# First weight sums of two projections one step sooner, and the last mix's weights split ahead of the projection's end

## The chip, the cores and the metric

The kernel runs on one core of a Trainium2 chip. The core has a matrix engine (PE, with its weight loads shown apart as PEld), a vector engine (DVE), a scalar engine (ACT), a general engine (POOL) and DMA queues, most of whose transfers are issued by SP. Each engine works through its own queue of instructions in order; semaphores tie the queues together. The metric is the device time of one execution in microseconds.

## The reference

Two transformer blocks follow each other on 1024 tokens of width 1024, all in fp32. Of the first block the pool layer matters here, of the second the MLP:

```python
def multiscale_pool(u):                 # windows 2, 4, 8, 16 for four groups of 256 columns
    ...
        outs.append((c[:, 1:] - lower) / count - uf[:, :, gi])

def pool_layer(h, w_in, w_mix, scale, w_out):
    B, S, _ = h.shape
    u, z = jnp.split(h @ w_in, [POOL_WIDTH], axis=-1)        # 1024 -> 2048
    p = multiscale_pool(u)
    m = jnp.einsum('bsgc,gcd->bsgd', p, w_mix).reshape(B, S, POOL_WIDTH) * scale
    return (m * jax.nn.silu(z)) @ w_out
...
        m = rms_norm(h, norm_mlp[l])
        h = h + jnp.square(jax.nn.relu(m @ w_up[l])) @ w_down[l]     # 1024 -> 4096 -> 1024
```

Ahead of the pool layer stands a sliding window attention layer, ahead of the MLP a layer of neighbourhood attention and a gated recurrence.

## The kernel before, in words

**Matrix products.** A product of fp32 matrices is made of three matmuls: each operand is split into a rounded part ("hi") and the remainder ("lo"), and `mm3` adds hi by hi (L108), hi by lo and lo by hi (L110 and L111). So each operand of PE needs a cast, made by ACT, and a subtraction for the remainder, made by DVE (`split_evac`, L118 and L119) or by POOL (`split_w`, L79 and L80; `split_group`, L275 and L276; `split_b`, L118 with L119 on POOL). PE's output goes to one of eight banks, which ACT or DVE empties.

**Seven products in place of eight.** The large products are cut into 2 x 2 blocks and made from seven block products, with sums of blocks as operands: A11, A12, then S2, S1, S3, S4 and A22. The sums of blocks are made by DVE, of activations and of weights.

**`project_pairs`** (L327) makes a projection from 1024 columns in this way, in pairs of 128-column blocks of weights. It is used twice: for the pool layer's `w_in` (8 pairs, called at L959 with `NF` = 5) and for the MLP's `w_up` (16 pairs, called at L1912 with `NF` = 4). Pair p takes the products A11 and A12 first (`first_two`), then S2, S1, S3, S4 and A22 (`pair`). The weight sums of a pair are made from its raw weights r1 and r2 by four subtractions (`weight_sums`): the first three yield the operand tt of S2 and S1 whose second half ends the chain; then ACT casts tt (L275), POOL makes the remainder (L276) and PE can start S2.

Before the pairs run, the second half of the tokens is turned by PE (`turned`, L282, into banks) and `sums(j)`, for j = 0 to 3, makes from two banks the activation sums S2, S1 (both from A21 and A22), S3 and S4 with their splits: about a dozen instructions on DVE and six on ACT for each step. Beside each step j of 1 to 3 PE runs the two opening products of pair j, whose raw weights `split_first` loads and splits; with `NF` = 5 pair 4's come behind the last step. In the kernel before, `load_raw(0, ...)` asks for pair 0's raw weights behind step `NF` - 3, that is 2 in the pool projection and 1 in the up projection, and `weight_sums` runs on them behind step 3. Raw weights and their splits live in three buffers each (`wraw`, `whi`, `wlo`).

**The pool layer behind its projection.** `Pooled` takes the projection's results: even pairs give u, which is pooled and split, odd pairs give z, which goes through silu. After each second pair `mix(g, q)` multiplies one group with its 256 x 256 weights `w_mix`: `w_rows` loads the weights into a `wraw` buffer and splits them, PE makes four banks of six matmuls, DVE scales each and multiplies it by z (L942), and the four blocks and their sums S1 to S4 go to memory (L956) and are loaded back later as `ub` (L1001) for the out projection. The last mix, `mix(GO[3], 3)` at L992, comes behind the last pair. Between them in the text stand the loads of the out projection's weights (w11, w21, w22, w12), the splits of its first activation blocks (L981 for the casts, DVE for the remainders, held back to the projection's end by `issue_after(ended[...])`) and `split_b(w11)`, whose remainders are made by POOL. The out projection begins with A11 and A12, whose last part comes from the last mix directly; the next product takes S2, which is loaded back from memory.

**Order.** A scheduler writes each engine's queue: it goes through the program as written and places an instruction according to what it needs and when buffers come free; `issue_after` adds an edge by which an instruction comes behind another. So moving lines in the text moves rows on several queues.

Of the kernel before, what the change touches and what calls it, by code (L numbers as in the profile page):

```python
# [23 lines left out]
KT = D // P  # L24
# [6 lines left out]
def fused_kernel(tc, a, out, stop=None, dbg=None):  # L31
# [51 lines left out]
    def cols(w, c0):  # L83
        return (lambda r: r.rearrange("p (k c) -> p k c", k=KT), w[:, c0:c0 + P].rearrange("(k p) c -> p k c", p=P))
# [164 lines left out]
    def split_b(b_):  # L249
        res = []  # L250
        for i in range(2):
            hi, lo = [wpool.tile([P, 1024], F32R, name=n).rearrange("p (k c) -> p k c", k=2) for n in ("whi", "wlo")]
            split_evac(hi, lo, b_[i], nc.gpsimd)
            res.append((hi, lo))
        return res
# [71 lines left out]
    def project_pairs(w, col, npr, xx, sh, gcol, rows, a11, a12, stage, raw_tile, opened, res, w0, scaled, NF):  # L327
# [39 lines left out]

        def split_first(p):
            r_ = load_w(cols(w, col(p, 0))).rearrange("p (k c) -> p k c", k=KT)
            hv, lv = [wpool.tile([P, 1024], F32R, name=m).rearrange("p (k c) -> p k c", k=KT) for m in ("whi", "wlo")]  # L370
            for sl in (LO, HI):
                split_evac(hv[:, sl], lv[:, sl], r_[:, sl])
            wf[p] = hv, lv

        with tc.issue_after(scaled):
            split_first(1)

        def sums(j):
# [14 lines left out]
            h, l = xx.at(4 + j, H1)  # L393
            nc.scalar.activation(out=h, in_=pb, func=AF.Copy, scale=gb)
            fused(l, pb, gb, f(h), ALU.subtract)
            split_evac(sh[3][0][:, j, :], sh[3][1][:, j, :], s3)
# [4 lines left out]
            nc.vector.tensor_tensor(out=s2, in0=a_, in1=s2, op=ALU.subtract)  # L401
            split_evac(sh[4][0][:, j, :], sh[4][1][:, j, :], s2)

        banks = {0: [turned(rows[4:], k) for k in (0, 4)]}
        for j in range(4):
            if j < 3:
                banks[j + 1] = [turned(rows[4:], j + 1 + k) for k in (0, 4)]
            if 0 < j < NF:
                open_[j] = first_two(j, wf[j])
            sums(j)  # L410
            if j + 2 < NF:
                split_first(j + 2)
            if j + 3 == NF:
                r0 = [load_raw(0, i) for i in range(2)] + [raw()]
        ready = {1: weight_sums(*r0)}
# [390 lines left out]
    with ExitStack() as ph:  # L806
# [34 lines left out]
        class Pooled:  # L841
# [44 lines left out]
            def last(self, p, ps):  # L886
                c_ = self.dst(p, "21")
# [45 lines left out]
        def mix(g, q):  # L933

            wm, pp = w_rows(w_mix[g], 0, 2, 0, 256), pooled.pp.pop(q)
# [41 lines left out]
        with tc.issue_after(ended[0]):  # L977
# [6 lines left out]
            ops = split_b(w11)  # L984
# [1072 lines left out]
```

## Time and profile before

| | |
|---|---|
| Median of 3 runs | 2407.47 us (2406.76 to 2408.1) |
| Profiled execution, its own time | 2405.66 us |
| Its span on the core | 2403.8 us |
| Mean granted PE clock | 0.982 |
| Pool projection, first pair's preparation | 474 to 505 us of the span |
| Last mix and out projection | 670 to about 815 us |
| Up projection, first pair's preparation | 1767 to 1795 us |

The profile is of one execution; times count from the start of its span. A row of the timeline gives start, duration, engine, line, operation, output and inputs by the program's names, shapes, and how many instructions the row stands for; in brackets the engine's idle time before it and what released it. In the view of waits a row tells for one engine and line what it waited for, the total, how often, and the longest. Matmuls overlap: a row's duration is longer than the distance to the next start, and the distance is what one costs.

### The profile page before, as it was taken

What the parts mean: (1) busy time and instruction counts of PE and PEld (TensorE: products, weight loads), DVE (VectorE), ACT (ScalarE), POOL (GpSimd) and SP (SyncE); (2) the same over time, 40 slices, a digit from 0 to 9 for tenths busy, and PEclk for the clock granted to TensorE, in tenths of its full rate; (3) what the DMA queues carried; (4) which work ended last, traced back from release to release, by engine and by line L of the source; (5) the groups of instructions that cost most, each with busy time, mean ns of one, the idle gap of its engine ahead of it and who ended that gap; (6) DMA issues with size and microseconds to landing.
All of it is one profiled execution on the core that took longest, in us unless ns stands there. A gap on an engine that the chain in (4) does not pass through costs nothing. (4 is left out here: it accounts for less than half of the span.)

```text
span 2403.8 us, 32250 instructions
## 1 busy us (share of the span) xinstructions
PE 2293.1 (95%) x11910; PEld 1905.2 (79%) x11910; DVE 1509.5 (63%) x2730; ACT 1022.2 (43%) x1921; POOL 805.2 (33%) x529
## 2 busy tenths in 40 slices
PE   7999999989978999999999999999979999999997
PEld 6878778767767888888988888877768888888886
DVE  5566676787668355454165656759884444687775
ACT  5344451633335445454232322323565555533334
POOL 2112133234433244342122112126414444454455
PEclk9999999989989999999999999999989999999999
DMA  5111113423372322211111111358135444664331
GB/s 158 36 27 36 28 36 106 152 54 118 101 250 71 101 58 53 58 54 58 42 47 49 53 54 46 123 185 291 61 123 180 162 146 165 246 240 159 113 123 70
DMA packets 249230, 254.41 MB, mean 106 GB/s; under 512 B 61096, under 2 KB 183038, under 8 KB 244848
## 3 DMA queue, kind: packets, MB, share of 16 engines
q1 hardware_dynamic: 240256, 234.69, 30.1%
q10 hardware_dynamic: 8224, 16.00, 1.7%
q0 software_dynamic: 592, 1.65, 0.4%
q8 instruction: 94, 1.54, 0.3%
q14 instruction: 64, 0.52, 0.1%
HBM read 182.05 MB, written 70.25 MB: 105 GB/s over the span
## 5 line engine op out<-in xcount | busy, mean ns | idle before, releaser
L108 PE MATMUL mm<-xh,whi 128*128 128x512 f32 (+2 forms) x1616 | 622.1, 385 | 11.7 <-DVE z L226 2.6
L110 PE MATMUL mm<-xl,whi 128*128 128x512 f32 (+2 forms) x1616 | 615.7, 381 | 0.0
L111 PE MATMUL mm<-xh,wlo 128*128 128x512 f32 (+2 forms) x1616 | 612.7, 379 | 1.2 <-POOL wlo L80 1.2
L80 POOL TENSOR_TENSOR wlo<-wraw,whi 128x1024 fp32r<-128x1024 f32 (+1 forms) x99 | 238.6, 2413 | 730.2 <-ACT whi L79 668.0
L108 PEld LDWEIGHTS mm<-xh,whi 128*128 128x128 f32 x1616 | 305.9, 189 | 69.2 <-DVE z L226 3.6
L111 PEld LDWEIGHTS mm<-xh,wlo 128*128 128x128 f32 x1616 | 305.9, 189 | 59.7 <-POOL wlo L80 1.9
L110 PEld LDWEIGHTS mm<-xl,whi 128*128 128x128 f32 x1616 | 306.2, 189 | 51.0
L111 PE MATMUL mm<-whi,xl 128*128 128x512 f32 (+1 forms) x752 | 274.6, 365 | 0.0
L79 ACT CAST whi<-wraw 128x1024 fp32r<-128x1024 f32 (+1 forms) x99 | 101.2, 1023 | 263.8 <-PE mm L110 145.5
L110 PE MATMUL mm<-wlo,xh 128*128 128x512 f32 (+1 forms) x560 | 196.8, 351 | 2.4 <-POOL wlo L80 1.4
L108 PE MATMUL mm<-whi,xh 128*128 128x512 f32 (+1 forms) x560 | 197.1, 352 | 1.8 <-DVE x L504 1.0
L110 PE MATMUL mm<-wlo,xl 128*128 128x512 f32 x416 | 165.9, 399 | 9.5 <-POOL wlo L119 9.5
L108 PE MATMUL mm<-whi,xl 128*128 128x512 f32 x416 | 165.9, 399 | 9.5 <-DVE r L132 6.0
L276 POOL TENSOR_TENSOR wlo<-raw,whi 128x1024 fp32r<-128x1024 f32 (+1 forms) x59 | 123.2, 2089 | 131.1 <-ACT whi L275 131.0
L111 PEld LDWEIGHTS mm<-whi,xl 128*128 128x128 f32 x752 | 143.9, 191 | 22.4
L119 POOL TENSOR_TENSOR wlo<-wraw,whi 128x1024 fp32r<-128x1024 f32 x36 | 102.2, 2846 | 116.5 <-ACT whi L118 111.0
L110 PEld LDWEIGHTS mm<-wlo,xh 128*128 128x128 f32 x560 | 105.7, 189 | 17.0 <-POOL wlo L80 2.0
L108 PEld LDWEIGHTS mm<-whi,xh 128*128 128x128 f32 x560 | 105.8, 189 | 16.4 <-DVE x L504 1.4
L276 POOL TENSOR_TENSOR wlo<-wraw,whi 128x1024 fp32r<-128x1024 f32 (+1 forms) x28 | 68.9, 2466 | 146.2 <-ACT whi L275 118.7
L108 PEld LDWEIGHTS mm<-whi,xl 128*128 128x128 f32 x416 | 80.3, 193 | 28.8 <-ACT ea L1017 6.4
L110 PEld LDWEIGHTS mm<-wlo,xl 128*128 128x128 f32 x416 | 80.1, 193 | 28.1 <-POOL wlo L119 11.5
L1979 DVE TENSOR_TENSOR X<-X,mm 128x512 f32<-128x512 f32 x112 | 73.1, 681 | 37.5 <-PE mm L111 37.5
(435 smaller groups left out, 4583.6 us busy)
## 6 DMA issues: line engine op xcount, KB each, us to landing
wraw<-in_w_in_dram SPq DMA_DIRECT2D x48, 512.0 KB, 3.7
d_S<-st SPq DMA_DIRECT2D x64, 256.0 KB, 4.6
raw<-in_w_up_dram SPq DMA_DIRECT2D x30, 512.0 KB, 5.4
d_A<-st ACTq DMA_DIRECT2D x48, 256.0 KB, 2.0
fa<-d_S SPq DMA_DIRECT2D x10, 1024.0 KB, 4.6
fa<-d_A SPq DMA_DIRECT2D x9, 1024.0 KB, 5.8
wraw<-in_attn_w_in_dram SPq DMA_DIRECT2D x32, 256.0 KB, 3.0
xh<-in_w_down_dram SPq DMA_DIRECT2D x16, 512.0 KB, 5.4
```

The source lines that it names most:

```text
L79: nc.scalar.copy(out=hv[:, i:i + n], in_=view[:, i:i + n])
L80: nc.gpsimd.tensor_tensor(out=lv[:, i:i + n], in0=view[:, i:i + n], in1=f(hv[:, i:i + n]), op=ALU.subtract)
L108: nc.tensor.matmul(ps, lhsT=lh[0], rhs=rh[0], start=first and i == 0, stop=False, skip_group_check=chain)
L110: nc.tensor.matmul(ps, lhsT=lh[0], rhs=rh[1], start=False, stop=False, skip_group_check=chain)
L111: nc.tensor.matmul(ps, lhsT=lh[1], rhs=rh[0], start=False, stop=last and i == n - 1, skip_group_check=chain)
L119: return (lo_eng or nc.vector).tensor_tensor(out=lo, in0=src, in1=f(hi), op=ALU.subtract)
L276: nc.gpsimd.tensor_tensor(out=lv, in0=view, in1=f(hv), op=ALU.subtract)
L1979: added[:] = [nc.vector.tensor_tensor(out=dst, in0=dst, in1=banks[t], op=ALU.add)]
```

## The change

It has three parts.

1. In `project_pairs` the loads for `split_first` stand apart (`load_first`), and those of pairs 1 to 3 are asked for at the start. Pair 0's raw weights are asked for behind step 0, pairs 2 and 3 are split there, and pair 4 behind step 1. `weight_sums` runs behind step 2. `sums(j)` does the part that S2 and S1 need and returns the rest (the second half of A22's split, S3's split, S4's subtraction and split) as a function `rest`; it is called at once for j = 0 to 2, and for j = 3 behind the weight sums and the loop. The subtraction for S4 now goes through `vec` and so shows as L226 in place of L401.
2. The last mix's weights are loaded and split in `Pooled.last`, ahead of the last pair's last evacuation, in place of in `mix`.
3. `split_b` takes an engine; w11's remainders are made by DVE, in place of POOL, and not ahead of the last addition of the projection.

```diff
--- before.py
+++ after.py
@@ -246,11 +246,11 @@
             made[:] = [split_evac(t_[:, 2 * i:2 * i + 2, :], t_[:, 4 + 2 * i:6 + 2 * i, :], parts[i])]
         return t_
 
-    def split_b(b_):
+    def split_b(b_, eng=nc.gpsimd):
         res = []
         for i in range(2):
             hi, lo = [wpool.tile([P, 1024], F32R, name=n).rearrange("p (k c) -> p k c", k=2) for n in ("whi", "wlo")]
-            split_evac(hi, lo, b_[i], nc.gpsimd)
+            split_evac(hi, lo, b_[i], eng)
             res.append((hi, lo))
         return res
 
@@ -365,13 +365,20 @@
 
         open_, wf = {0: first_two(0, w0)}, {}
 
+        wr = {}
+
+        def load_first(p):
+            wr[p] = load_w(cols(w, col(p, 0))).rearrange("p (k c) -> p k c", k=KT)
+
         def split_first(p):
-            r_ = load_w(cols(w, col(p, 0))).rearrange("p (k c) -> p k c", k=KT)
+            r_ = wr.pop(p)
             hv, lv = [wpool.tile([P, 1024], F32R, name=m).rearrange("p (k c) -> p k c", k=KT) for m in ("whi", "wlo")]
             for sl in (LO, HI):
                 split_evac(hv[:, sl], lv[:, sl], r_[:, sl])
             wf[p] = hv, lv
 
+        for p in (1, 2, 3):
+            load_first(p)
         with tc.issue_after(scaled):
             split_first(1)
 
@@ -390,16 +397,21 @@
             split_evac(sh[2][0][:, j, :], sh[2][1][:, j, :], s2)
             fused(a21, pb, gb, a21, ALU.add)
             split_evac(*xx.at(j, H1), a21)
-            h, l = xx.at(4 + j, H1)
-            nc.scalar.activation(out=h, in_=pb, func=AF.Copy, scale=gb)
-            fused(l, pb, gb, f(h), ALU.subtract)
-            split_evac(sh[3][0][:, j, :], sh[3][1][:, j, :], s3)
+
+            def rest():
+
+                h, l = xx.at(4 + j, H1)
+                nc.scalar.activation(out=h, in_=pb, func=AF.Copy, scale=gb)
+                fused(l, pb, gb, f(h), ALU.subtract)
+                split_evac(sh[3][0][:, j, :], sh[3][1][:, j, :], s3)
+                vec(s2, a_, s2, ALU.subtract)
+                split_evac(sh[4][0][:, j, :], sh[4][1][:, j, :], s2)
+
             h, l = xx.at(4 + j, H0)
             a_, there = a12(j)
             if not there:
                 nc.gpsimd.tensor_tensor(out=a_, in0=f(h), in1=f(l), op=ALU.add)
-            nc.vector.tensor_tensor(out=s2, in0=a_, in1=s2, op=ALU.subtract)
-            split_evac(sh[4][0][:, j, :], sh[4][1][:, j, :], s2)
+            return rest
 
         banks = {0: [turned(rows[4:], k) for k in (0, 4)]}
         for j in range(4):
@@ -407,12 +419,22 @@
                 banks[j + 1] = [turned(rows[4:], j + 1 + k) for k in (0, 4)]
             if 0 < j < NF:
                 open_[j] = first_two(j, wf[j])
-            sums(j)
-            if j + 2 < NF:
-                split_first(j + 2)
-            if j + 3 == NF:
-                r0 = [load_raw(0, i) for i in range(2)] + [raw()]
-        ready = {1: weight_sums(*r0)}
+            rest = sums(j)
+            if j < 3:
+                rest()
+            if j == 0:
+                split_first(2)
+                split_first(3)
+                if NF > 4:
+                    load_first(4)
+                r0 = [load_raw(0, i) for i in range(2)]
+            if j == 1:
+                if NF > 4:
+                    split_first(4)
+                r0.append(raw())
+            if j == 2:
+                ready = {1: weight_sums(*r0)}
+        rest()
         for p in range(4, NF):
             open_[p] = first_two(p, wf[p])
         opened()
@@ -884,6 +906,8 @@
                     self.steps()
 
             def last(self, p, ps):
+                if p == 7:
+                    self.wm = w_rows(w_mix[GO[3]], 0, 2, 0, 256)
                 c_ = self.dst(p, "21")
                 if p % 2:
                     ended[:] = [nc.scalar.activation(out=c_, in_=ps, func=AF.Silu).ins, added[0].ins]
@@ -932,7 +956,7 @@
 
         def mix(g, q):
 
-            wm, pp = w_rows(w_mix[g], 0, 2, 0, 256), pooled.pp.pop(q)
+            wm, pp = pooled.wm if q == 3 else w_rows(w_mix[g], 0, 2, 0, 256), pooled.pp.pop(q)
             zs = [pooled.t.pop((2 * q + 1, j)) for j in range(2)]
             m = {(j, h): zs[j][:, h * 512:h * 512 + 512] for j in range(2) for h in range(2)}
             for j, h in ((0, 0), (1, 0), (0, 1), (1, 1)):
@@ -981,7 +1005,8 @@
                 nc.scalar.copy(out=h_, in_=r_)
                 with tc.issue_after(ended[1]):
                     vec(l_, r_, f(h_), ALU.subtract)
-            ops = split_b(w11)
+            with tc.issue_after(ended[1]):
+                ops = split_b(w11, nc.vector)
         X = Rows([raw_tile().rearrange("p k c -> p (k c)") for _ in range(4)], None, None)
 
         def load_x(h, ch):
```

Line numbers move by some twenty: L385, L401, L942 and L981 before are L392, L226, L966 and L1005 after.

DVE's queue in the pool projection, at the third and fourth step of the sums (`fused` is L385 before and L392 after; `wraw<-wraw` is a weight sum of pair 0; `ea<-ea,mm` adds the opening products of a pair). Before:

```order
L401 TENSOR_TENSOR u<-u 128x512
L119 TENSOR_TENSOR wlo<-wraw,whi 128x512
L385 SCALAR_TENSOR_TENSOR z<-mm,vecs,sum 128x512
L119 TENSOR_TENSOR s4l<-u,s4h 128x512
L226 TENSOR_TENSOR ea<-ea,mm 128x512
L385 SCALAR_TENSOR_TENSOR sum<-mm,vecs,z 128x512
L385 SCALAR_TENSOR_TENSOR z<-mm,vecs,z 128x512
L119 TENSOR_TENSOR s3l<-z,s3h 128x512
L119 TENSOR_TENSOR s2l<-sum,s2h 128x512
L119 TENSOR_TENSOR xl_5018<-z,xh_5017 128x512
L385 SCALAR_TENSOR_TENSOR xl_5018<-mm,vecs,xh_5017 128x512
L401 TENSOR_TENSOR sum<-sum 128x512
```

After:

```order
L226 TENSOR_TENSOR u<-u 128x512
L226 TENSOR_TENSOR wraw<-wraw 128x512
L392 SCALAR_TENSOR_TENSOR z<-mm,vecs,sum 128x512
L119 TENSOR_TENSOR s4l<-u,s4h 128x512
L226 TENSOR_TENSOR wraw<-wraw 128x512
L226 TENSOR_TENSOR ea<-ea,mm 128x512
L226 TENSOR_TENSOR wraw<-wraw 128x512 x2
L392 SCALAR_TENSOR_TENSOR sum<-mm,vecs,z 128x512
L392 SCALAR_TENSOR_TENSOR z<-mm,vecs,z 128x512
L119 TENSOR_TENSOR s3l<-z,s3h 128x512
L119 TENSOR_TENSOR s2l<-sum,s2h 128x512
```

Pair 0's four weight sums stand among the first rows of the last step; before, the first of them came right behind the rows shown. The splits of the opening weights (`wlo<-wraw,whi`) moved ahead of this place.

ACT's queue at the end of the last pair and the last mix (L876 and L889 before, L898 and L913 after, are the evacuations of the last pair; L79 is the cast of the mix's weights; `whi<-wraw` at L118 are w11's). Before:

```order
L876 COPY z<-mm 128x512 x2
L882 ACTIVATE z<-z 128x512 x2
L889 ACTIVATE z<-mm 128x512
L981 CAST xh_6331<-raw 128x1024
L981 CAST xh_6331<-raw 128x512
L981 CAST xl_6332<-raw 128x1024
L981 CAST xl_6332<-raw 128x512
L118 CAST whi<-wraw 128x1024 x2
L79 CAST whi<-wraw 128x512
```

After:

```order
L898 COPY z<-mm 128x512
L79 CAST whi<-wraw 128x512
L898 COPY z<-mm 128x512
L904 ACTIVATE z<-z 128x512 x2
L913 ACTIVATE z<-mm 128x512
L1005 CAST xh_6337<-raw 128x1024
L1005 CAST xh_6337<-raw 128x512
L1005 CAST xl_6338<-raw 128x1024
L1005 CAST xl_6338<-raw 128x512
L118 CAST whi<-wraw 128x1024 x2
```

The cast of the mix's weights went from behind w11's to between two evacuations of the last pair.

DVE's queue at the same place (`raw` holds the activation blocks loaded back, `w` is in w21, w22 and w12's sums, L942 and L966 are the four results of the last mix, `sum<-z` is its S2). Before:

```order
L226 TENSOR_TENSOR xh_6331<-raw,xh_6331 128x512
L226 TENSOR_TENSOR xl_6332<-raw,xl_6332 128x1024
L226 TENSOR_TENSOR xl_6332<-raw,xl_6332 128x512
L241 TENSOR_TENSOR w_6326<-w_6326,w_6325 128x1024 x2
L942 SCALAR_TENSOR_TENSOR z<-mm,vecs,z 128x512 x2
L119 TENSOR_TENSOR xh_6331<-z,xh_6331 128x512
L942 SCALAR_TENSOR_TENSOR z<-mm,vecs,z 128x512
L119 TENSOR_TENSOR xl_6332<-z,xl_6332 128x512
L226 TENSOR_TENSOR z<-z 128x512
L942 SCALAR_TENSOR_TENSOR z<-mm,vecs,z 128x512
L226 TENSOR_TENSOR z<-z 128x512
L226 TENSOR_TENSOR sum<-z 128x512
```

After:

```order
L226 TENSOR_TENSOR xh_6337<-raw,xh_6337 128x1024
L226 TENSOR_TENSOR xh_6337<-raw,xh_6337 128x512
L226 TENSOR_TENSOR xl_6338<-raw,xl_6338 128x1024
L226 TENSOR_TENSOR xl_6338<-raw,xl_6338 128x512
L119 TENSOR_TENSOR wlo<-wraw,whi 128x1024 x2
L119 TENSOR_TENSOR xh_6337<-z,xh_6337 128x512
L966 SCALAR_TENSOR_TENSOR z<-mm,vecs,z 128x512 x3
L119 TENSOR_TENSOR xl_6338<-z,xl_6338 128x512
L226 TENSOR_TENSOR z<-z 128x512
L241 TENSOR_TENSOR w_6332<-w_6332,w_6331 128x1024
L226 TENSOR_TENSOR z<-z 128x512
L226 TENSOR_TENSOR sum<-z 128x512
```

w11's two remainders are in DVE's queue now, and the two L241 rows, ahead of the mix's results before, went to between the sums and behind S2 (the second is the row after the last one shown).

## The prediction

> **What bounds the kernel now.** I read the page's first table, then PE's waits, then the granted clock by stretch, then the rows round each long wait.
>
> ```profile
> span 2403.8 us, 32250 instructions
> PE 2293.1 (95%) x11910; PEld 1905.2 (79%) x11910; DVE 1509.5 (63%) x2730; ACT 1022.2 (43%) x1921; POOL 805.2 (33%) x529
> ```
>
> PE is busy for 95% of the span, so a change that gives it no less work can only win back PE's idle time, and the clock it loses behind idle time. The view of waits (engine, line, waited for: us in total, times, longest) between 440 and 820 us, where the pool layer runs, and between 1750 and 2080 us, where the up projection runs, holds the waits that the edits touch:
>
> ```profile
> PE mm L108 <- ACT whi L79: 6.0, 1, 6.0
> PE mm L108 <- DVE r L132: 6.0, 1, 6.0
> PE mm L111 <- POOL wlo L80: 5.7, 1, 5.7
> PE mm L108 <- ACT whi L275: 5.2, 1, 5.2
> ```
> ```profile
> PE mm L108 <- ACT whi L275: 9.5, 1, 9.5
> ```
>
> The L275 waits are for pair 0's first weight sums (place A in the pool projection, place B in the up projection). The L79 and L80 waits are for the last mix's weights, and the 6.0 under r L132 comes in the out projection behind it (place C). The windows view (start:end, then length and busy time of PE, PEld, DVE, ACT, POOL, then PEclk, DMA share, GB/s) shows what comes after such waits:
>
> ```profile
> 496.00:513.00 17.00, 10.58 (x31) 7.63 (x30) 14.28 (x18) 4.66 (x8) 6.36 (x3) 0.70 0.06 15
> 604.00:612.00 8.00, 6.12 (x28) 4.72 (x27) 6.67 (x8) 4.11 (x6) 2.61 (x2) 1.00 0.23 67
> 670.00:690.00 20.00, 8.30 (x24) 5.78 (x23) 12.53 (x10) 7.17 (x10) 8.29 (x3) 0.66 0.48 163
> ```
>
> The clock falls to 0.70 and 0.66 behind the waits of A and C, and stays at 1.00 over the 1.88 us wait in the middle row (its row is below). Full-rate starts of matmuls lie 0.23 us apart, half-rate ones 0.43; so 13 half-rate ones behind A's wait cost 2.5 us, and 10 behind C's second wait 2.0.
>
> **Place A: pair 0's sums one step sooner.** Columns: start, duration, engine, operation, count, idle time before.
>
> ```profile
> 606.84 0.50 PE L108 MATMUL mm<-s2h,whi 128*128 128x512 f32 x1 [1.88 <-ACT z L876]
> 473.89 0.69 DVE L401 TENSOR_TENSOR u<-u 128x512 f32<-128x512 f32 x1
> 500.02 2.02 DVE L226 TENSOR_TENSOR wraw<-wraw 128x512 f32<-128x512 f32 x3
> 501.46 2.51 ACT L275 CAST whi<-wraw 128x1024 fp32r<-128x1024 f32 x3 [2.51 <-DVE wraw L226]
> 502.56 0.79 PE L108 MATMUL mm<-s2h,whi 128*128 128x512 f32 x1 [5.21 <-ACT whi L275]
> 502.59 6.36 POOL L276 TENSOR_TENSOR wlo<-wraw,whi 128x1024 fp32r<-128x1024 f32 x3 [12.99 <-ACT whi L275]
> 504.99 0.80 PE L111 MATMUL mm<-s2h,wlo 128*128 128x512 f32 x1 [1.21 <-POOL wlo L276]
> ```
>
> The chain is: third weight sum on DVE (second of the three at 500.02, done about 501.4), cast on ACT, remainder on POOL (2.4 us after 502.59, at 504.99), and PE's first matmul with wlo. DVE works without a break from 473.89 to 501.4: 41 instructions in 27.5 us, 0.67 each. In the changed order 32 stand ahead of the same sum, since what the last step defers goes behind it; 9 fewer is 6.0 us, so the sum ends near 495.4. But ACT must first evacuate that step's first product, and PE now comes later: two subtractions for weights stand ahead of the additions that free the transposes' bank, 2 x 0.67 less slack, which I put at 1.15 us. PE's last opening product then ends at 498.7 instead of 497.35 (502.56 less 5.21), and the cast starts near 496.7, 4.8 us sooner. wlo is there at 500.2, again 4.8 sooner. PE waits about 1 us, less than the 1.88 us that left the clock alone, so the 2.5 us of half rate goes too. **A: 4.8 + 2.5 = 7.3.** Bounds: 8.9 if both waits and the half rate go entirely (5.21 + 1.21 + 2.5), 2 if ACT's cast gains only about half and the clock still falls. What DVE defers (S3's and S4's remainders) is needed by products that PE starts only after S2 and S1, some 96 matmuls or 22 us later, which hides it. The raw weights are asked for earlier from a queue that moves 15 GB/s in that stretch, at no cost that I can see.
>
> **Place B: the same code in the up projection.**
>
> ```profile
> 1766.23 0.69 DVE L401 TENSOR_TENSOR st<-fa,st 128x512 f32<-128x512 f32 x1
> 1769.51 0.50 PE L108 MATMUL mm<-xh,whi 128*128 128x512 f32 x1 [1.25 <-ACT st L388]
> 1790.17 1.29 DVE L226 TENSOR_TENSOR wraw<-wraw 128x512 f32<-128x512 f32 x2
> 1792.07 6.38 POOL L276 TENSOR_TENSOR wlo<-wraw,whi 128x1024 fp32r<-128x1024 f32 x3 [55.46 <-ACT whi L275]
> 1794.48 0.79 PE L111 MATMUL mm<-s2h,wlo 128*128 128x512 f32 x1 [1.27 <-POOL wlo L276]
> ```
>
> From 1766.23 to the end of the third sum (first of the two at 1790.17, done at 1790.85) DVE has 37 instructions; 29 are left ahead of it, 8 x 0.67 = 5.3 us sooner. The addition that frees the bank stands behind three more instructions, so PE's first product of that step starts up to 2 us later and DVE waits some 0.6 us of it out: 5.3 - 0.6 = 4.7, and POOL's remainder and the matmul at 1794.48 move with it. PE still waits here, over 4 us in all, so the half rate behind it (6 matmuls, 1.2 us) stays. **B: 4.7.** Bounds: 12.0 (9.53 + 1.27 + 1.2) and 1.5, if the later bank costs DVE all of its 2 us and another 2.
>
> **Place C: the last mix's weights, and w11's remainder on DVE.**
>
> ```profile
> 670.13 0.39 PE L111 MATMUL mm<-xh,wlo 128*128 128x512 f32 x1
> 675.87 0.62 ACT L79 CAST whi<-wraw 128x512 fp32r<-128x512 f32 x1
> 681.14 2.24 POOL L80 TENSOR_TENSOR wlo<-wraw,whi 128x512 fp32r<-128x512 f32 x1
> 683.44 0.79 PE L111 MATMUL mm<-sum,wlo 128*128 128x512 f32 x1 [5.68 <-POOL wlo L80]
> 690.91 0.39 PE L108 MATMUL mm<-whi,xh 128*128 128x512 f32 x1
> 712.03 0.39 PE L108 MATMUL mm<-whi,xl 128*128 128x512 f32 x1
> 715.32 0.50 PE L110 MATMUL mm<-wlo,xl 128*128 128x512 f32 x1 [2.22 <-POOL wlo L119]
> 744.76 0.77 PE L108 MATMUL mm<-whi,xl 128*128 128x512 f32 x1 [5.99 <-DVE r L132]
> 672.12 1.83 DVE L226 TENSOR_TENSOR xh<-raw,xh 128x1024 fp32r<-128x1024 f32 x2 [3.59 <-ACT xh L981]
> 673.87 1.82 DVE L226 TENSOR_TENSOR xl<-raw,xl 128x1024 fp32r<-128x1024 f32 x2
> 675.60 6.66 DVE L241 TENSOR_TENSOR w<-w,w 128x1024 f32<-128x1024 f32 x2
> 694.93 0.68 DVE L226 TENSOR_TENSOR sum<-z 128x512 f32<-128x512 f32 x1
> 695.64 0.32 SPq L956 DMA_DIRECT2D d_mS<-sum  x1
> 701.36 0.80 SPq L1001 DMA_DIRECT2D ub<-d_mS  x2
> 706.21 2.00 ACT L118 CAST xl<-ub 128x1024 fp32r<-128x1024 f32 x2 [4.00 <-DMA ub<-d_mS]
> 711.95 6.64 POOL L119 TENSOR_TENSOR wlo<-wraw,whi 128x1024 fp32r<-128x1024 f32 x2 [11.83 <-ACT whi L118]
> 739.58 3.29 DVE L119 TENSOR_TENSOR xl<-ub,xl 128x1024 fp32r<-128x1024 f32 x1
> 743.95 0.67 DVE L226 TENSOR_TENSOR z<-z,mm 128x512 f32<-128x512 f32 x1
> ```
>
> The mix's cast (0.62 us) and its remainder (2.24) move to about 661-663, ahead of the last evacuation; both fit beside PE's last product. PE runs on from 670.5: 24 matmuls x 0.23 end the mix at 676.0, where now the out projection starts at 690.91. w11's two remainders cost DVE 1.2 us each (the 1024-column part of the 1.83 row) in place of 6.1 on POOL and come about 677, a wait of half a microsecond. So PE is 14 us ahead there. It cannot keep them. Its first out products (690.91 to 712.03, 21.1 us) would end near 697.7, and the next one needs S2, which goes through DRAM: sum at 694.93, store, load at 701.36, cast at 706.21, POOL at 711.95, matmul at 715.32. That is 19.7 us from the sum's end to the matmul, and the change touches none of it. How much sooner is the sum? By PE alone, 681 (4.7 us after the mix, as now). By DVE, from 672.1: 3.65 for the four subtractions, 2.4 for w11, 3.3 for the half of L241 ordered ahead, nine 128x512 operations at 0.7: 15.7 us, so 688. I take 688, since all of these stand in its queue ahead of the sum: PE resumes at 688 + 19.7 = 707.7, after a **new wait of about 10 us** at the S2 product, with half rate behind it as now.
>
> From there to 744.76 PE now takes 29.4 us, 23.5 of them work and 5.99 the wait for a bank, which the addition at 743.95 frees. The second half of xl's remainder (3.29) and one addition (0.8 with its gap) go behind it: 29.4 - 4.1 = 25.3, so the gate opens at 733.0. **C: 744.76 - 733.0 = 11.7**. Bounds: 25.6 if the four waits (6.01, 5.68, 2.22, 5.99) and the half rate behind them (5.7) all go; 4 if the sum is no earlier and only DVE's 4.1 us are saved.
>
> The wait at that gate is then about 1.8 us, and I leave the 2.1 us of half rate behind it in. The Trainium skill ("TensorE: Matmul & The Clock Gate", section "HAM oscillation") says 'The abstract rule is "no PE-idle gaps >~3.4µs."' By that rule the 2.1 us go as well and the time would be 2381.7. But behind the 1.25 us wait at 1769.51 ten matmuls ran at half rate, so this trace does not bear the rule out and I do not use it.
>
> **Sum.** 7.3 + 4.7 + 11.7 = 23.7. The profiled execution's 2403.8 becomes 2380.1. The median lies 3.67 above that span: **2383.8 us**.
>
> **Rivals.** *More is kept:* S2's sum comes when PE allows, at 681. Then PE resumes at 700.7, C is 18.7, and the time 2376.8. For it: most of DVE's remainders could run while PE mixes; against it: the order puts them first. *Less is kept:* C's wait comes back nearly whole at the S2 product, because POOL's and DVE's work collide (the 6.66 us for two L241 is 3.3 each), the sum stays at 695, C is 4 and A and B at 60%: 11, or 2396. *Slower:* PE falls to half rate at 676 and the short waits that follow keep it there, so the 216 matmuls up to the gate take 0.20 us more each: 43 - 23.7 = 19 slower, 2427. It decides from about 120 such matmuls. Against it: after each wait seen, the clock came back within 6 to 13 matmuls. *It does not do what it says:* the sums are not sooner because the raw weights land late; the order shows them asked for a whole step ahead, and then only C is left, 2396.
>
> **Chances.** Forecast, 2378 to 2391: 0.60. More kept: 0.14. Less kept, or C alone: 0.19. No change 0.03; slower 0.04. The range 2373 to 2397 takes in both neighbours and leaves out the bounds' far corners. What a measurement of this kernel can tell from no change is about 0.2%, 4.8 us; so faster 0.93, same 0.03, slower 0.04.
>
> **What would show it.** In A a wait of about 1 us before the S2 product and the clock above 0.9 there; in B the wait of 9.53 down to 3 to 5; the L275 casts near 496.7 and, in the old count, 1786. In C no wait at the mix, a wait of 8 to 11 us some 27 us after the mix began, released by POOL's wlo at L119, and the gate's wait near 2. It is wrong if the clock stays low between them, or if a wait appears after 760 us, where I expect every product to move unchanged.

## The result, and the profile after

| | before | after |
|---|---|---|
| Median | 2407.11 us (4 runs) | 2394.57 us (4 runs, 2391.29 to 2395.45) |
| Ratio of the times | | 0.9946, 95% interval 0.9929 to 0.9963 |
| Span of the profiled execution | 2403.8 us | 2393.6 us |

The change makes the kernel 12.5 us faster, and by the interval between 8.9 and 17.1. The forecast was faster by 23.7, to 2383.8. The direction held and the size is half: 2394.57 lies inside the wide range of 2373 to 2397, but outside the 2378 to 2391 that the forecast gave most of its chance. The page's first lines, after:

```profile
span 2393.6 us, 32247 instructions
PE 2290.5 (96%) x11910; PEld 1904.0 (80%) x11910; DVE 1509.4 (63%) x2732; ACT 1021.5 (43%) x1921; POOL 802.7 (34%) x527
```

PE has the same 11910 matmuls. To see where time went, the same matmul is looked up in both executions and its starts compared; a negative shift means earlier than before.

| Matmul | before | after | shift |
|---|---|---|---|
| pool projection, ahead of place A | 440.16 | 440.57 | +0.4 |
| A: pair 0, S2, first matmul with wlo | 504.99 | 500.50 | -4.5 |
| A: pair 0, S3, first | 512.87 | 505.63 | -7.2 |
| A: pair 1, S2, second | 521.26 | 521.90 | +0.6 |
| mix of the first group | 540.11 | 537.91 | -2.2 |
| last pair, S3 | 660.46 | 658.30 | -2.2 |
| C: out projection, second product | 701.84 | 685.29 | -16.6 |
| C: product with S2, first with wlo | 715.32 | 706.24 | -9.1 |
| C: product behind the bank's wait | 744.76 | 734.07 | -10.7 |
| ahead of B | 1691.79 | 1681.93 | -9.9 |
| B: pair 0, S2, first matmul with wlo | 1794.48 | 1780.04 | -14.4 |
| B: pair 1, A22, first | 1820.82 | 1809.84 | -11.0 |
| last matmul | 2390.32 | 2380.12 | -10.2 |

At each of the three places a gain appears that is about as large as forecast, and part of it, in A nearly all, is gone a few microseconds later. In A and B the view of PE's waits (engine, line, waited for: total, times, longest) names what took it back; first 440 to 820 us, then 1750 to 2080 us:

```profile
PE mm L108 <- ACT whi L118: 7.0, 1, 7.0
...
PE mm L108 <- DVE u L226: 5.4, 2, 5.0
PE mm L108 <- DVE w L128: 5.0, 1, 5.0
```
```profile
PE mm L108 <- DVE st L1853: 3.6, 3, 2.6
PE mm L108 <- ACT whi L275: 3.2, 1, 3.2
```

The waits of 6.0 us for L79 and 5.7 for L80 are gone; that for L275 is 3.2 us in place of 9.5 in B, and there is none in A. The waits for DVE's u (L226) and st (L1853, L1828 before) were 0.5 and 0.8 us in all before: these are additions, by which DVE takes a product out of a bank that PE's next product needs. The 7.0 us is the wait for S2 that the forecast had put at about 10.

**Place A after**, from the timelines of PE, DVE and POOL:

```profile
500.50 0.50 PE L111 MATMUL mm<-s2h,wlo 128*128 128x512 f32 x1 [1.34 <-POOL wlo L276]
505.63 0.39 PE L108 MATMUL mm<-s3h,whi 128*128 128x512 f32 x1
516.19 0.79 PE L108 MATMUL mm<-xh,whi 128*128 128x512 f32 x1 [4.95 <-DVE u L226]
509.15 0.68 DVE L226 TENSOR_TENSOR raw<-raw 128x512 f32<-128x512 f32 x1
509.92 2.86 DVE L226 TENSOR_TENSOR wraw<-raw 128x512 f32<-128x512 f32 x1
512.82 2.71 DVE L226 TENSOR_TENSOR wraw<-raw,wraw 128x512 f32<-128x512 f32 x1
515.46 0.67 DVE L226 TENSOR_TENSOR u<-u,mm 128x512 f32<-128x512 f32 x1
509.86 2.39 POOL L276 TENSOR_TENSOR wlo<-wraw,whi 128x1024 fp32r<-128x1024 f32 x1 [4.90 <-ACT whi L275]
512.21 2.77 POOL L276 TENSOR_TENSOR wlo<-raw,whi 128x1024 fp32r<-128x1024 f32 x1
```

The matmul at 516.19 is the first of pair 0's last product, A22, which goes into a bank that this addition has to read first; it starts at 515.46. (The expectations below call that product pair 1's first; it is pair 0's A22.) Ahead of it in DVE's queue stand pair 2's weight sums, which nobody needs for another pair's length. The first takes 0.68 us, the next two 2.86 and 2.71: both began after a subtraction on POOL had begun, and end 0.5 us behind its end (POOL 512.25 and 514.98, DVE 512.78 and 515.53). That is what is seen if DVE does nothing while POOL works and then takes its usual time. DVE had stood still beside the remainders of pair 0 before the change too; new are the 4.2 us beside those of pair 1, which before found DVE idle and waiting for PE. The Trainium skill ("SBUF — State Buffer", section "SBUF: two separate sides") says that an operation of GpSimd and a DVE operation with two inputs in SBUF share a pair of ports as an exclusive lock, held for the whole instruction. These rows agree with that, and group_dve below bears it out: without POOL's subtractions the same rows take 0.69 us.

**Place B after** shows the same pattern at pair 0's A22: a weight sum stretched from 0.68 to 2.71 us beside POOL's subtraction, the addition right behind it, and PE's matmul. At pair 1's A22, 16 us later, additions again stand behind weight sums of a later pair; here one of them waits 1.18 us for its raw weights from memory:

```profile
1789.30 2.84 POOL L276 TENSOR_TENSOR wlo<-wraw,whi 128x1024 fp32r<-128x1024 f32 x1 [1.77 <-ACT whi L275]
1789.97 2.71 DVE L226 TENSOR_TENSOR wraw<-raw 128x512 f32<-128x512 f32 x1
1792.61 0.67 DVE L1853 TENSOR_TENSOR st<-st,mm 128x512 f32<-128x512 f32 x1
1793.34 0.50 PE L108 MATMUL mm<-xh,whi 128*128 128x512 f32 x1 [0.69 <-DVE st L1853]
1807.17 0.69 DVE L226 TENSOR_TENSOR wraw<-raw 128x512 f32<-128x512 f32 x1 [1.18 <-DMA raw<-in_w_up_dram]
1809.11 1.28 DVE L1853 TENSOR_TENSOR st<-st,mm 128x512 f32<-128x512 f32 x2
1809.84 0.50 PE L108 MATMUL mm<-xh,whi 128*128 128x512 f32 x1 [2.60 <-DVE st L1853]
```

**Place C after:**

```profile
681.35 2.88 DVE L226 TENSOR_TENSOR z<-z 128x512 f32<-128x512 f32 x1
684.14 0.68 DVE L226 TENSOR_TENSOR sum<-z 128x512 f32<-128x512 f32 x1
690.66 0.79 SPq L1026 DMA_DIRECT2D ub<-d_mS  x2
697.11 1.99 ACT L118 CAST xl<-ub 128x1024 fp32r<-128x1024 f32 x2 [5.53 <-DMA ub<-d_mS]
706.24 0.80 PE L110 MATMUL mm<-wlo,xl 128*128 128x512 f32 x1 [0.82 <-POOL wlo L119]
729.37 3.30 DVE L119 TENSOR_TENSOR xl<-ub,xl 128x1024 fp32r<-128x1024 f32 x1
734.07 0.76 PE L108 MATMUL mm<-whi,xl 128*128 128x512 f32 x1 [5.02 <-DVE w L128]
```

S2's sum ends at 684.8 in place of 695.6, and its way through memory to PE's first matmul with wlo takes 21.4 us where it took 19.7: the load now takes 6.5 us from its issue to the cast, where it took 4.9. So of the 14 us that PE had gained at the mix, 7 were left. And at the bank behind it a remainder of 3.30 us, beside POOL's subtraction, still stands ahead of the addition, as it did before:

```profile
728.89 2.70 POOL L119 TENSOR_TENSOR wlo<-w,whi 128x1024 fp32r<-128x1024 f32 x1 [5.86 <-ACT whi L118]
```

### The profile page after: what moved, and what is told of

It reads as the page before. It is cut to its first block, busy times and chain, and to the rows that moved or that the text cites. A ratio compares the mean times of both kernels' runs of the same rounds, so it can differ in the third digit from the quotient of the medians.

```text
span 2393.6 us, 32247 instructions
## 1 busy us (share of the span) xinstructions
PE 2290.5 (96%) x11910; PEld 1904.0 (80%) x11910; DVE 1509.4 (63%) x2732; ACT 1021.5 (43%) x1921; POOL 802.7 (34%) x527
## 5 line engine op out<-in xcount | busy, mean ns | idle before, releaser
L80 POOL TENSOR_TENSOR wlo<-wraw,whi 128x1024 fp32r<-128x1024 f32 (+1 forms) x99 | 235.8, 2385 | 739.9 <-ACT whi L79 676.0
L79 ACT CAST whi<-wraw 128x1024 fp32r<-128x1024 f32 (+1 forms) x99 | 101.1, 1023 | 264.0 <-PE mm L110 146.0
L110 PE MATMUL mm<-wlo,xl 128*128 128x512 f32 x416 | 164.5, 396 | 10.7 <-POOL wlo L119 10.7
L119 POOL TENSOR_TENSOR wlo<-wraw,whi 128x1024 fp32r<-128x1024 f32 x34 | 95.3, 2807 | 103.4 <-ACT whi L118 98.0
L226 DVE TENSOR_TENSOR st<-st 128x512 f32<-128x512 f32 x64 | 63.2, 1008 | 56.7 <-ACT st L1928 55.6
```

The lines of the kernel that those rows point to most:

```text
L79: nc.scalar.copy(out=hv[:, i:i + n], in_=view[:, i:i + n])
L80: nc.gpsimd.tensor_tensor(out=lv[:, i:i + n], in0=view[:, i:i + n], in1=f(hv[:, i:i + n]), op=ALU.subtract)
L110: nc.tensor.matmul(ps, lhsT=lh[0], rhs=rh[1], start=False, stop=False, skip_group_check=chain)
L119: return (lo_eng or nc.vector).tensor_tensor(out=lo, in0=src, in1=f(hi), op=ALU.subtract)
L226: return nc.vector.tensor_tensor(out=out_, in0=x_, in1=y_, op=op)
```

## The experiments

All ran with the kernel before beside them, whose median lay between 2407.1 and 2408.6; differences from the changed kernel are between medians. Each kernel ran 4 to 10 times, and its executions spread over 2 to 9 us, so where two intervals overlap, the difference of the two kernels is not certain. Line numbers in rows are each kernel's own.

| Kernel | median | ratio to before, 95% |
|---|---|---|
| changed kernel | 2394.57 | 0.9946 (0.9929 to 0.9963) |
| only_mix | 2400.12 | 0.9969 (0.9957 to 0.9981) |
| only_sums | 2401.26 | 0.9975 (0.9965 to 0.9985) |
| mix_pool | 2398.78 | 0.9965 (0.9953 to 0.9977) |
| sums_behind_adds | 2391.32 | 0.9934 (0.9919 to 0.9949) |
| s2_first | 2391.39 | 0.9933 (0.9918 to 0.9948) |
| group_dve | 2389.35 | 0.9923 (0.9908 to 0.9938) |
| adds_s2 | 2389.44 | 0.9925 (0.9910 to 0.9940) |
| adds_s2_x | 2389.18 | 0.9925 (0.9908 to 0.9941) |
| all_four | 2391.75 | 0.9934 (0.9922 to 0.9947) |
| group_s2_x | 2385.72 | 0.9907 (0.9893 to 0.9920) |
| all_four_p3 | 2385.76 | 0.9905 (0.9890 to 0.9920) |
| out_dve | 2380.64 | 0.9894 (0.9878 to 0.9910) |

### The parts of the change alone

**only_mix** is the kernel before with the second and third part of the change: the hunks of its diff at `split_b`, `Pooled.last` and `mix`, and none in `project_pairs`.

> The projection helper as before; only the last mix's weights are split ahead of the last pair's end and w11's remainders go to DVE. Theory (the gain is made at the mix, the earlier sums gave theirs back): 8 us faster than before, 2399, with no wait at the mix, a wait of 6 to 8 us at the product that takes S2 and one of about 5 us at the bank behind it. Rival (the three parts gained evenly, and each place gave the same share): 4 us faster, 2403.

7.2 us faster than before. The wait at the mix is gone and that at S2 is 8.1 us, as expected. The expected wait of 5 us at the bank behind it did not come: the remainder ahead of the addition took 1.20 us here, because it began 0.06 us ahead of POOL's subtraction, and this time POOL was the slow one, with 4.02 us:

```profile
732.87 1.20 DVE L119 TENSOR_TENSOR xl<-ub,xl 128x1024 fp32r<-128x1024 f32 x1
732.93 4.02 POOL L119 TENSOR_TENSOR wlo<-w,whi 128x1024 fp32r<-128x1024 f32 x1 [3.02 <-ACT whi L118]
```

**only_sums** is the reverse: the hunks in `project_pairs` alone.

> Only the earlier weight sums and the sums' last step in two parts; the mix as before. Theory: 2 to 3 us faster than before, 2404.5, with the wait ahead of S2 down to 1.3 us in the pool projection, PE 7 us ahead at S3, and a new wait of about 5 us at the next pair's first product, released by an addition on DVE; the same in the up projection with 2.6 us. Rival: 8 us faster, 2399, and the new waits of the changed kernel came from the mix's part.

6.0 us faster than before (3.6 to 8.4), between the two expectations. The new waits are there without the mix's part, so the rival's reason for them falls:

```profile
PE mm L108 <- DVE u L226: 5.2, 2, 5.0
```

In its profiled execution (span 2402.1) the first part wins only 1.7 us. Executions of this kernel lie between 2398.2 and 2404.6, and what makes them differ is told in the last section. 6.0 and 7.2 make 13.2, the changed kernel's 12.5 within the uncertainty: the parts act apart.

Of the first part, the function `rest` moves nothing: with the last step's sums kept in one piece, each of the five queues holds the same operations in the same order as in the changed kernel. What moves the queues is that loads and weight sums stand earlier in the text.

**mix_pool** is only_mix without the third part.

```diff
-            with tc.issue_after(ended[1]):
-                ops = split_b(w11, nc.vector)
+            ops = split_b(w11)
```

> The kernel before with the last mix's weights split ahead of the last pair's end alone; w11's remainders stay on POOL. Theory (PE's lead at the mix is given back at S2, whose sum and way through memory decide): a wait of 2 to 4 us for w11's remainder appears ahead of the out projection, the wait at S2 shrinks by as much, and the time is that of only_mix, 2400. Rival (POOL's work beside DVE delays S2's sum): 3 to 4 us slower than only_mix, 2403.5.

2398.8, the same as only_mix within the uncertainty. A wait of 1.6 us for w11's remainder appears ahead of the out projection, and the wait at S2 falls from 8.1 to 6.6:

```profile
PE mm L108 <- ACT whi L118: 6.6, 1, 6.6
```

So what the third part wins ahead of S2, S2 takes back; by itself it is worth nothing here.

### The order of additions and weight sums

**sums_behind_adds** puts pair 2's and later opening pairs' weight sums behind an addition:

```diff
                 if p + 1 < NF:
-                    ready[p + 1] = done
+                    ready[p + 1] = added[0].ins if p else done
```

> The changed kernel, but the weight sums of pair 2 and the later opening pairs stand in DVE's queue behind the additions of the pair before, as those of the remaining pairs do. Theory (the additions that free PE's banks are held by weight sums that stand ahead of them and run at 2.7 to 2.9 us each beside POOL): the wait of 4.95 us at pair 1's first product falls below 2 and its half-rate matmuls go, the 2.6 us wait in the up projection falls too; 5 to 8 us faster than the changed kernel, 2388. Rival (DVE has more work there than PE, whatever the order): the wait only moves to pair 2's S2 product or its neighbours; within 2 us of the changed kernel, 2394.

3.3 us faster than the changed kernel by the medians, with intervals that overlap. The trace divides it by place. In B the theory holds: no wait at pair 0's and pair 1's A22, and a shift of -15.1 us at the latter, in place of -11.0. In A it holds at first. The wait of 4.95 us is gone; two others come later, at pair 1's A22 and at the first group's mix, but they cost less:

```profile
526.89 0.50 PE L108 MATMUL mm<-xh,whi 128*128 128x512 f32 x1 [2.77 <-DVE z L226]
532.75 2.07 PE L108 MATMUL mm<-sum,whi 128*128 128x512 f32 x4 [2.40 <-ACT sum L118]
```

In A the additions of pair 1 then stand behind the pooling of u, which follows at once and is wide (128x1039). The up projection has no such work. At 560 us the shift is still -8.3, where the changed kernel's is -2.2 (some 2 us of the difference are the clock at 478 us, told in the last section). Then PE waits 3.2 us at the second group's mix for ACT's cast of the pooled u (0.3 in the changed kernel); weight sums of a later pair stand among that pooling on DVE now. At the last pair's S3 -4.2 are left. So in the end the rival holds in A: what is won in the first pairs is mostly given back, though later than it said.

### POOL's subtractions

**group_dve** gives the remainders of the first two pairs' weights to DVE:

```diff
+            e_ = nc.gpsimd if p > 1 else nc.vector
-            g = split_group(tt, KT)
+            g = split_group(tt, KT, e_)
```

and likewise for r2 and r1.

> The changed kernel, but the weight remainders of pairs 0 and 1 in both projections are made by DVE, in place of POOL. Theory (DVE's operations on two operands in SBUF stand still while POOL subtracts: 2.7 to 2.9 us in place of 0.68): the rows of 2 to 2.9 us in the pool projection's first two pairs go, 8 us of DVE time, for 6 us of added remainders at 1.2 us; the wait of 4.95 us at pair 1's first product falls to 1 to 3 us; 1 to 4 us faster than the changed kernel, 2392. Rival (the amount of work on DVE decides, not POOL): the wait grows by the added 6 us, 2399.

5.2 us faster than the changed kernel (the intervals overlap a little), more than the theory said and against a rival that made it slower, although DVE has some 6 us more to do in each projection. Pair 2's weight sums in A, and the addition behind them:

```profile
507.93 0.69 DVE L226 TENSOR_TENSOR wraw<-raw 128x512 f32<-128x512 f32 x1
508.65 0.69 DVE L226 TENSOR_TENSOR wraw<-raw,wraw 128x512 f32<-128x512 f32 x1
509.87 1.22 DVE L276 TENSOR_TENSOR wlo<-wraw,whi 128x1024 fp32r<-128x1024 f32 x1
511.62 0.69 DVE L226 TENSOR_TENSOR u<-u,mm 128x512 f32<-128x512 f32 x1 [0.54 <-PE mm L111]
502.35 0.50 PE L111 MATMUL mm<-s2h,wlo 128*128 128x512 f32 x1 [3.71 <-DVE wlo L276]
```

The same two sums take 0.69 us each, and the addition waits for PE and not the other way round. In exchange the first wait of A is longer, 3.71 us in place of 1.34, since pair 0's remainder comes behind other work in DVE's queue. More of what A wins now stays: the shift is -6.6 us at 560, where the changed kernel's is -2.2 (1 us of the difference is there at 485 already).

### S2's way to the out projection

**s2_first** takes the sums in the order S3, S2, S1, S4:

```diff
-                                      ("S1", m[0, 1], ...), ("S2", s2, ...),
+                                      ("S2", s2, ...), ("S1", m[0, 1], ...),
```

> The changed kernel, but the last of each mix's sums are taken and stored in the order S3, S2, S1, S4. Theory (the 7.0 us wait at the S2 product is the sum's place in DVE's queue plus a round trip through memory that nothing shortens): the sum ends 3 to 3.5 us sooner, the wait falls to about 4, and the bank's wait behind it keeps part: 2 to 3.5 us faster than the changed kernel, 2391.5. Rival (the wait is set by the load's own queue or by the weights' sums): no change, 2394.5.

3.2 us faster by the medians, with intervals that overlap, but the trace does not show it where the theory put it. The wait at S2 is 6.3 us in place of 7.0: the row of 2.88 us beside POOL is now the S2 sum itself.

```profile
679.94 2.88 DVE L226 TENSOR_TENSOR sum<-z 128x512 f32<-128x512 f32 x1
```

What did fall is the wait at the bank behind it, from 5.0 to 1.2 us, because the remainder of 3.30 us ahead of the addition is a 1.21 in this execution, POOL being idle at that moment.

**adds_s2** puts sums_behind_adds and s2_first together.

> The changed kernel with both reorderings tried singly: weight sums of the opening pairs behind the additions of the pair before, and S2 ahead of S1 in the last sums. Theory (they act at different places): their gains add up, 6 us faster than the changed kernel, 2388.5. Rival (what one wins the other's place gives back): 2391.5, as each alone.

5.1 us faster than the changed kernel: most of the sum of both (6.4), and not to be told from either expectation by these runs.

**adds_s2_x** also holds the later loads of x behind those of S2 and S1:

```diff
-        load_x(0, 1)
+        with tc.issue_after(s2_in):
+            load_x(0, 1)
```

and likewise for the two loads of the lower half.

> As adds_s2, with the later loads of the residual x asked for behind the loads of S2 and S1. Theory (the way of S2 through memory now shares the queue with x: 6.5 us from the load's issue to its cast, 4.9 in the kernel before): the load lands 1.5 to 2 us sooner, the wait at the S2 product falls by as much, 1.5 us faster than adds_s2, 2387. Rival (x then comes too late for the additions that free the banks): the wait moves to the product behind, no change or up to 3 us slower, 2388.5 to 2391.5.

No difference in the medians from adds_s2 (2389.2 and 2389.4). In the traces the wait at S2 is 5.3 us in place of 5.9, less than the 1.5 to 2 of the theory. Inconclusive by time.

### Together

**all_four** joins adds_s2_x and group_dve; **group_s2_x** is the same without sums_behind_adds; **all_four_p3** is all_four with the remainders of pairs 0 to 3 on DVE.

> The changed kernel with the four edits that helped singly: remainders of pairs 0 and 1 on DVE, opening pairs' weight sums behind the additions, S2 ahead of S1 in the last sums, the later x loads behind the loads of S2 and S1. Theory (the first two act on one place, DVE's queue in the first pairs, the last two on another): 5 us from the first two together and 5 from the last two, 2384.5. Rival (all of it adds up): 2379; other rival (the additions and the remainders on DVE push each other back): 2389, as each alone.

> As all_four without the weight sums moved behind the additions. Theory: once POOL no longer holds DVE, the order of sums and additions matters little; the pool projection is the same within 1 us, the up projection 1 to 2 us slower, 2385.5. Rival (the order matters by itself): 3 to 5 us slower than all_four, 2388.5.

> As all_four, with the remainders of pairs 0 to 3 on DVE in place of 0 and 1. Theory (POOL's subtractions stop DVE wherever DVE is the later engine, and in the pool projection it is that up to pair 3): 1 to 3 us faster than all_four, 2382.5. Rival (from pair 2 on DVE has slack and 1.2 us more on it for each remainder only delays the additions): 1 to 3 us slower, 2386.5.

all_four falls to the rival that the edits push each other back: 2391.8, worse than group_dve alone. group_s2_x, which differs by one line, is 6.0 us better, against an expected 1 us worse. So once POOL no longer holds DVE in the first pairs, moving weight sums behind the additions costs more than it brings. In all_four's trace (an execution 6.5 us above its median) PE waits at two places by the second group's mix, 560 to 585 us:

```profile
PE mm L108 <- ACT sum L118: 3.3, 1, 3.3
PE mm L108 <- DVE z L226: 2.8, 1, 2.8
```

In group_s2_x's trace the first of them is 0.4. This wait of 3.2 or 3.3 us is in sums_behind_adds, adds_s2 and adds_s2_x too, so it goes with that order and not with the engine of the remainders; what the order gains lies in the first pairs, where group_dve's edit has won it already. The gains of the two do not add, and this price stays. With pairs 2 and 3 on DVE as well the time is 2385.8, 6 us below all_four, in the direction of the theory for POOL but more than it said, and the wait of 3.3 us is gone; against group_s2_x it is no gain.

**out_dve** is group_s2_x with the five other `split_b` of the pool layer's out projection on DVE too:

```diff
-        ops = split_b(w21)
+        ops = split_b(w21, nc.vector)
```

> As group_s2_x, with all weight remainders of the pool layer's out projection made by DVE in place of POOL. Theory (beside POOL's subtractions DVE loses more than the 1.2 us each remainder costs it): the waits of 1.5 us for POOL's remainder at S2 and 1.9 us two products later go, and the time is 2 to 4 us below group_s2_x, 2382.5. Rival (from S2 on DVE is the engine that sets the time there, so added work on it counts in full): ten remainders at 1.2 us reappear at the banks' waits, up to 6 us slower, 2389.

2380.6, 27 us below the kernel before (22 to 29 by the interval): the best of all, and better than both kernels of the case. It is 5.1 us below group_s2_x by the medians, but single executions of the two overlap (2378.3 to 2387.5, and 2382.8 to 2388.8). The traces agree at the place itself: from the last pair's S3 to 820 us the shift grows by 15.9 us here and by 11.1 in group_s2_x. The waits at S2, 4.9 and 1.5 us in group_s2_x, are down to 1.1, with no further edit to S2's way except that POOL is silent:

```profile
675.08 0.68 DVE L226 TENSOR_TENSOR sum<-z 128x512 f32<-128x512 f32 x1
692.60 0.50 PE L110 MATMUL mm<-wlo,xl 128*128 128x512 f32 x1 [1.11 <-DVE wlo L119]
```

The windows view from 670 to 770 us (length, busy time and instructions of PE, PEld, DVE, ACT, POOL, then clock, DMA share, GB/s) bears on why, for group_s2_x and then for out_dve:

```profile
670.00:770.00 100.00, 89.41 (x386) 71.23 (x386) 84.41 (x110) 51.04 (x95) 32.97 (x14) 0.93 0.44 157
```
```profile
670.00:770.00 100.00, 92.94 (x410) 75.32 (x409) 84.90 (x144) 54.98 (x103) 4.73 (x2) 0.97 0.47 170
```

DVE is busy for 84 to 85 us in both and does 144 instructions in it in place of 110: the ten remainders, at 1.22 us each, and 24 of later work that now comes sooner. The time for them it had before spent standing still beside POOL, and the profile counts that as busy. Part is given back: behind the out projection PE now waits 4.1 us for DVE's raw (L308), a wait that group_s2_x does not have.

## Why the prediction was right or wrong

**What bounds the kernel** was read rightly: PE's work did not change, and all that was won is idle time and half-rate matmuls.

**Place A (forecast 7.3 us).** The chain of the weight sums went as worked out: the matmul with wlo 4.5 us sooner (forecast 4.8), a wait of 1.34 us (about 1), the clock unbroken from there to S3, and 7.2 us won at S3. The step that failed is the sentence on what DVE defers, that it "is needed by products that PE starts only after S2 and S1, some 96 matmuls or 22 us later, which hides it". Two things are wrong in it. A product of this projection is 12 matmuls, so the cover is 24 of them: from 498.5 to 505.6. That was still enough for the deferred splits: S3 shows no wait. What was not looked at is what comes after them on DVE: the additions that free the banks, behind the next pairs' weight sums, some of them at 2.7 to 2.9 us. The slow row was in the trace of before (a weight sum of 2.84 us at 504.97), but there it lay beside PE's half-rate stretch, and DVE then waited 3.05 and 1.96 us for PE ahead of the two additions. Ending PE's wait took that slack away. What stays of A is some 2.6 us in the profiled execution (from +0.4 to -2.2), and even this only through two later waits: at pair 1's S2 all was gone (+0.6), and behind it a wait of 1.30 us at pair 1's S4 is no longer there and one of 2.66 at the first group's mix is 1.87.

**Place B (forecast 4.7).** The same: -9.9 ahead, -14.4 at the matmul with wlo, so 4.5 us won as forecast, then taken back to about 1 by the waits at pair 0's and pair 1's A22 (0.69 and 2.60 us). At the second a weight sum ahead of the addition had waited for its raw weights, so POOL's part in it is not shown. Nothing of this was in the sum or in a rival. The forecast had named a wait after 760 us, where it expected every product to move unchanged, as a sign of being wrong; these two are such waits. By the times, A and B together are worth 6.0 us (3.6 to 8.4), half of the 12.0 forecast.

**Place C (forecast 11.7).** The mechanism was right up to the bank: no wait at the mix, the lead given back at S2, a wait of 7.0 + 0.8 us where about 10 was forecast, and w11's remainders on DVE in time. S2's matmul came 6.9 us sooner than A's shift explains (forecast 7.6), with the longer way through memory (21.4 against 19.7 us) made up by an earlier sum. The term that was mis-sized is the 4.1 us that DVE was to save ahead of the bank: it was 1.6, because the remainder of 3.3 us stayed ahead of the addition, and the wait there is 5.0 and not 2. How much of this term is kept hangs on which of POOL and DVE begins first: with the same edit, only_mix has the remainder at 1.20 and no wait there. C is worth 8.5 in the trace and 7.2 by the time.

**The rivals.** "Less is kept" named the collision of POOL's and DVE's work, but only for S2's sum in C, where it took about 2 us; the same collision in A and B, where it decided, was not priced. Its time, 2396, lies close to the 2394.6 measured, but it was reached with C at 4 us and A and B at 60%, where C kept 7.2 and A and B half; that is luck in part. A clock that stays low up to the gate did not come: from 670 to 690 us, at 0.66 before, the granted clock is 1.00 after, and from 704 to 734, up to the gate, 0.90.

**The sentence on the clock** left the half rate behind the gate's wait in the sum, against the Trainium skill's rule; the wait was 5.0 us, so this place tells nothing on the rule.

## What to carry to other kernels

When a wait of the bounding engine is removed, follow the helping engine's queue for one or two products more: what it had finished in the shadow of that wait comes next, and its slack is gone. Where an operation of a helping engine lasts several times its usual time, its busy time is not work; look for the other engine that is active in the same rows, and try moving that engine's work onto the slowed one before easing its load. And an order that wins a few microseconds at one bottleneck can cost as much further on; once that bottleneck is gone, only the cost is left.

## What the runs showed of the hardware

**DVE stands still beside POOL.** DVE operations of 128x512 with two inputs in SBUF took 0.68 us alone and 2.7 to 2.9 us beside a POOL subtraction that reads SBUF; those that take one input from a bank did not slow down: three of L966 took 2.06 us together while POOL ran from 675.33 to 679.13. Where DVE began first, as in only_mix, POOL was the one that took longer, 4.02 us. So in group_dve and, less surely, in out_dve a remainder that POOL makes in 2.4 us or more was cheaper on DVE at 1.22 us, even where DVE was the busier engine; for w11's two (mix_pool) no difference was seen.

```profile
676.78 2.06 DVE L966 SCALAR_TENSOR_TENSOR z<-mm,vecs,z 128x512 f32<-128x512 f32 x3
675.33 3.80 POOL L119 TENSOR_TENSOR wlo<-w,whi 128x1024 fp32r<-128x1024 f32 x1 [15.18 <-ACT whi L118]
```

**The same wait does not always cost the clock.** Behind the same 2.30 us wait at 478 us, ten microseconds of the changed kernel's profiled execution had a granted clock of 0.66, and of sums_behind_adds', which is the same program up to there on PE, 1.00. First the changed kernel, then the other:

```profile
476.00:486.00 10.00, 7.71 (x22) 5.97 (x23) 8.91 (x16) 7.90 (x13) 4.12 (x2) 0.66 0.94 252
478.03 1.11 PE L282 MATMUL mm<-ident,raw 128*128 128x128 f32 x4 [2.30 <-DVE z L226]
```
```profile
476.00:486.00 10.00, 7.17 (x32) 5.71 (x33) 10.00 (x17) 7.88 (x13) 4.20 (x2) 1.00 0.93 248
478.10 0.66 PE L282 MATMUL mm<-ident,raw 128*128 128x128 f32 x4 [2.30 <-DVE z L226]
```

Ten half-rate matmuls cost about 2 us, and the changed kernel has ten waits of over 1 us between 470 and 820 us alone. That fits the spread of 2 to 9 us between executions of one kernel here, and may be why single traces and medians differ by 1 to 4 us in what a part is worth; that it is the whole of either is not shown. The Trainium skill ("TensorE: Matmul & The Clock Gate", section "HAM oscillation") names gaps over about 3.4 us; here one of 2.30 us sufficed in one execution and not in another.
